# Softmax over 16,384 rows on one core: group 4's scaling split in two on GpSimd, store 0 waiting for the first part

## The chip, the core and the metric

The kernel runs on one core of one Trainium2 chip. Its compute engines here are VectorE (DVE in the profile), ScalarE (ACT) and GpSimd (POOL); TensorE does nothing. SyncE (SP) only waits for semaphores and issues the DMAs, all on one queue, whose transfers are spread over the core's 16 DMA engines. The metric is the time of one execution on the device in microseconds; the kernel before took 159.41 us in the median of three runs (159.51, 159.41, 159.30).

## The reference

```python
x = randn(16, 1024, 512)  # float32

def reference(x):
    x_max = np.max(x, axis=-1, keepdims=True)
    exp_x = np.exp(x - x_max)
    return exp_x / np.sum(exp_x, axis=-1, keepdims=True)
```

It is a softmax over the last axis, in float32: 16 x 1024 = 16,384 rows of 512 numbers. 33.55 MB are read and as many written.

## The kernel before

The 16,384 rows stand as 128 rows of 512 numbers on each of 128 partitions. A *group* is 8 such rows (128 x 4096 numbers, 2 MB), so there are 16 groups, 0 to 15. All data lives in one tensor `held` in SBUF, a ring with room for 12 groups (line 16): groups 12 to 15 take the places of groups 0 to 3 once these are stored. What is loaded is changed in place and stored from there.

**Transfers.** The DMAs move *blocks* (line 21): of 16 rows, two groups, 4 MB, and one of 32 rows (64 to 95, groups 8 to 11), 8 MB. A load or store is named here by its first row: load 64 brings rows 64 to 95, store 0 takes rows 0 to 15, groups 0 and 1. `ORDER` (line 22) writes the order of all 14 transfers out by hand: loads 0, 16, 32, 48, 64; stores 0, 16, 32; loads 96, 112; stores 48, 64, 96, 112. SP issues them in this order on a single queue. The first five loads are issued at once. Ahead of every further one, lines 142 to 157 put waits: a store waits until the groups in it are scaled (one semaphore per group, `scaled[g]`); a load that reuses a place in the ring waits for the store that empties it; and `AFTER` (line 42) adds to four of them a wait for one more group. In this kernel store 0 has to wait for group 4, though it holds groups 0 and 1 only, load 96 for group 8, load 112 for group 9 and store 48 for group 11. A group that has been waited for once isn't waited for again (`done`). As SP takes its instructions in order, whatever stands behind a waiting one waits as well.

**Compute.** For each group g there are three steps.

- M: VectorE takes the maximum of each row, negated, into `shift` (line 168), after the load that brings the group.
- ScalarE computes exp(x + shift) row by row, eight instructions per group, and sums each row into `sums` (line 212).
- P or V: VectorE computes 1/sums (line 176), and the group is multiplied by it (line 182), on GpSimd for groups 0 to 11 (P) and on VectorE for groups 12 to 15 (V). The multiplication is a single instruction over 8 rows, `recip` broadcast along each row, and raises `scaled[g]` at its end.

`VECTOR` (line 46) gives the order of the steps on VectorE, written out by hand; GpSimd takes its groups in order, each after its reciprocal is there.

The one line of waits that the change touches:

```python
AFTER = {("S", 0): 4, ("L", 96): 8, ("L", 112): 9, ("S", 48): 11}
```

Of the kernel before, what the change touches and what calls it, by code (L numbers as in the profile page):

```python
# [13 lines left out]
GROUP = 8  # L14
# [24 lines left out]

AFTER = {("S", 0): 4, ("L", 96): 8, ("L", 112): 9, ("S", 48): 11}

# [28 lines left out]
@with_exitstack  # L74
def kernel(
    ctx: ExitStack,
    tc: tile.TileContext,
    x: bass.AP,
    out: bass.AP,
):  # L80
    nc = tc.nc
    nc.at_finalize(loads_at_the_head)
    P = nc.NUM_PARTITIONS

    d = x.shape[-1]
    x_rows, out_rows = x.flatten_outer_dims(), out.flatten_outer_dims()
    assert x_rows.shape[0] == GROUPS * GROUP * P

    def in_dram(rows, a, b):

        first, last = next(k for k in BLOCKS if k[0] <= a and b <= k[1])
        block = rows[first * P : last * P].rearrange("(p r) d -> p r d", p=P)
        return block[:, a - first : b - first, :]

    held = nc.alloc_sbuf_tensor("held", [P, RING, d], F32).ap()
    shift = nc.alloc_sbuf_tensor("shift", [P, GROUPS * GROUP], F32).ap()
    sums = nc.alloc_sbuf_tensor("sums", [P, GROUPS * GROUP], F32).ap()
    recip = nc.alloc_sbuf_tensor("recip", [P, GROUPS * GROUP], F32).ap()

    loads = [k for what, k in ORDER if what == "L"]  # L100
    stores = [k for what, k in ORDER if what == "S"]
    loaded = {k: nc.alloc_semaphore(f"loaded{k[0]}") for k in loads}
    scaled = [nc.alloc_semaphore(f"scaled{g}") for g in range(GROUPS)]
    stored = {k: nc.alloc_semaphore(f"stored{k[0]}") for k in stores}
    maxed = nc.alloc_semaphore("maxed")
    expd = nc.alloc_semaphore("expd")
    to_pool = nc.alloc_semaphore("to_pool")
    to_vector = nc.alloc_semaphore("to_vector")

    def take(engine, semaphore, n):  # L110

        engine.wait_ge(semaphore, n).then_inc(semaphore, -n)  # L112

    def rows(a, b):
        assert a // RING == (b - 1) // RING
        return held[:, a % RING : (b - 1) % RING + 1, :]

    def meets(k, a, b):
        return k[0] < b and a < k[1]

    def group(g):
        return g * GROUP, (g + 1) * GROUP

    def stats(t, g):
        return t[:, g * GROUP : (g + 1) * GROUP]

    def load(k):
        copy = nc.sync.dma_start(out=rows(*k), in_=in_dram(x_rows, *k))
        copy.then_inc(loaded[k], 16)
        return copy  # L130

    with tc.manual_schedule():
        for _, k in ORDER[:AHEAD]:
            tc.no_tile_sem_insts.add(load(k).ins.name)
    tc.close()
    tc.compile()  # L139

    taken, done = set(), set()
    for what, k in ORDER[AHEAD:]:
        for g in range(GROUPS):
            due = AFTER.get((what, k[0])) == g or (what == "S" and meets(k, *group(g)))
            if due and g not in done:
                take(nc.sync, scaled[g], 1)
                done.add(g)
        if what == "L":
            for s in stores:
                if meets(s, k[0] - RING, k[1] - RING) and s not in taken:  # L150
                    take(nc.sync, stored[s], 16)
                    taken.add(s)
            load(k)
        else:
            nc.sync.dma_start(out=in_dram(out_rows, *k), in_=rows(*k)).then_inc(
                stored[k], 16
            )

    seen, given = set(), {}

    def rowmax(g):
        for k in loads:
            if meets(k, *group(g)) and k not in seen:
                take(nc.vector, loaded[k], 16)
                seen.add(k)
        nc.vector.reduce_max(  # L168
            out=stats(shift, g), in_=rows(*group(g)), axis=AX, negate=True
        ).then_inc(maxed, 1)  # L170

    def scale(g, engine, ready):

        if g == 0:
            take(nc.vector, expd, 1)
        ratio = nc.vector.reciprocal(out=stats(recip, g), in_=stats(sums, g))  # L176
        if g:
            ratio.wait_op(expd, g, "sem-ge")
        ratio.then_inc(ready, 1)
        if g == 0:  # L180
            take(engine, ready, 1)
        product = engine.tensor_mul(  # L182
            out=rows(*group(g)),
            in0=rows(*group(g)),
            in1=stats(recip, g).unsqueeze(2).to_broadcast([P, GROUP, d]),
        )
        if g:
            given[ready] = given.get(ready, 0) + 1
            product.wait_op(ready, given[ready], "sem-ge")
        product.then_inc(scaled[g], 1)  # L190

    for step in VECTOR.split():
        what, g = step[0], int(step[1:])
        if what == "M":
            rowmax(g)
        elif what == "V":
            scale(g, nc.vector, to_vector)
        else:
            scale(g, nc.gpsimd, to_pool)
    take(nc.vector, expd, GROUPS - 1)  # L200
    take(nc.vector, to_vector, given[to_vector])
    take(nc.gpsimd, to_pool, given[to_pool])


    nc.scalar.preload_act_table(EXP)  # L205

    with nc.scalar.Fori(0, GROUPS) as i:  # L207
        take(nc.scalar, maxed, 1)
        for r in range(GROUP):
            row = held[:, bass.ds(i % (RING // GROUP) * GROUP + r, 1), :]  # L210
            at = bass.ds(i * GROUP + r, 1)
            act = nc.scalar.activation(  # L212
                out=row,
                in_=row,
                func=EXP,
                bias=shift[:, at],
                scale=1.0,
                accum_out=sums[:, at],
            )
        act.then_inc(expd, 1)  # L220


    for k in stores:
        if k not in taken:
            take(nc.sync, stored[k], 16)
# [30 lines left out]
```

## Time and profile before

| what | us |
|---|---|
| median of three timed runs | 159.41 |
| the profiled execution, its whole time | 159.34 |
| its span, first to last instruction | 158.0 |
| VectorE / ScalarE / GpSimd busy | 90.0 / 92.1 / 83.9 |
| one scaling of 128 x 4096 on GpSimd (line 182) | 7.018 |
| the same on VectorE | 4.424 |
| one row maximum of 128 x 4096 on VectorE (line 168) | 4.398 |
| one exp of 128 x 512 on ScalarE (line 212) | 0.707 |
| issue of store 0 / load 96 / load 112 / store 48 on SP | 58.56 / 86.53 / 93.50 / 107.38 |

The span is what the profile covers; around it lie another 1.3 us that belong to the execution's time. Times such as 58.56 count from the span's start. "Busy" is the time in which an engine has an instruction running. A DMA's issue is a short instruction on SP (shown as SPq); the transfer itself runs later, on the DMA engines, behind what was issued before it, and "to landing" is the time from the issue until its semaphore shows that all is there. Each of the 16 DMA engines moves its share of a transfer in packets of 32 KB (64 KB for the block of 32 rows); the trace has a start and a duration for every packet.

### The profile page before, as it was taken

The page shows a single profiled execution, that of the slowest core. Times are in us where ns is not written, and L with a number is a line of the kernel's source. Part 1 is how long each engine was busy: PE and PEld are TensorE (multiplying, and loading weights), DVE is VectorE, ACT ScalarE, POOL GpSimd, SP SyncE. Part 2 cuts the span into 40 slices and gives each one's busy share as a digit, 9 for nine tenths or more (in the row PEclk, how much of TensorE's full clock was granted, in tenths as well). Part 3 has the DMA queues.
Part 4 walks back from the last instruction along what each step waited for, and adds up shares of the span by engine and source line. Part 5 has one row for each costly group of instructions (what it writes and reads, how often), then busy time and mean ns, then how long its engine had stood idle before and what let it go on. Part 6 is the DMA issues. An engine that isn't in the chain of part 4 may idle for free. (4 is left out here: it accounts for less than half of the span.)

```text
span 158.0 us, 716 instructions
## 1 busy us (share of the span) xinstructions
DVE 90.0 (57%) x36; ACT 92.1 (58%) x257; POOL 83.9 (53%) x16
## 2 busy tenths in 40 slices
DVE  0008959778877915969770000695999996920000
ACT  1100699999999998399999300049946839000000
POOL 0000009999999999999999999991000000000000
DMA  8999999999969979999999999999999969999996
GB/s 265 423 481 423 398 456 465 406 415 481 564 265 531 481 315 398 423 481 423 398 448 465 406 406 398 415 498 415 398 448 481 531 265 531 390 406 406 465 456 265
DMA packets 2016, 67.11 MB, mean 425 GB/s; under 512 B 224, under 2 KB 224, under 8 KB 224
## 3 DMA queue, kind: packets, MB, share of 16 engines
q1 hardware_dynamic: 2016, 67.11, 99.1%
HBM read 33.55 MB, written 33.55 MB: 425 GB/s over the span
## 5 line engine op out<-in xcount | busy, mean ns | idle before, releaser
L212 ACT ACTIVATE held<-held,shift x128 | 90.4, 707 | 39.0 <-ACTq L112 39.0
L182 POOL TENSOR_TENSOR held<-held,recip 128x4096 f32<-128x4096 f32 x12 | 83.7, 7018 | 23.1 <-POOLq L112 23.1
L168 DVE TENSOR_REDUCE shift<-held 128x8 f32<-128x4096 f32 x16 | 70.2, 4398 | 27.7 <-DVEq L112 27.7
L212 ACT ACTIVATION_READ_ACCUMULATOR held<-held,shift x128 | 23.9, 187 | 0.0
L182 DVE TENSOR_TENSOR held<-held,recip 128x4096 f32<-128x4096 f32 x4 | 17.7, 4424 | 0.1
L176 DVE RECIPROCAL recip<-sums 128x8 f32<-128x8 f32 x16 | 3.2, 201 | 21.4 <-ACT held L212 19.5
L205 ACT ACT_TABLE_LOAD x1 | 1.3, 1283 | 3.4 <-PEq L139 3.4
L240 POOL MEMSET const-float32-0.0<- 128x1 f32 x1 | 0.1, 99 | 0.2 <-issue 0.2
L240 POOL MEMSET const-bfloat16-1.0<- 128x1 bf16 x1 | 0.1, 102 | 0.0
L240 POOL MEMSET const-uint8-127<- 128x1 uint8 x1 | 0.1, 102 | 0.0
L240 POOL MEMSET const-float32-1.0<- 128x1 f32 x1 | 0.1, 99 | 0.0
## 6 DMA issues: line engine op xcount, KB each, us to landing
held<-in_x_dram SPq DMA_DIRECT2D x6, 4096.0 KB, 18.7
out_dram<-held SPq DMA_DIRECT2D x6, 4096.0 KB, 19.8
held<-in_x_dram SPq DMA_DIRECT2D x1, 58.5
out_dram<-held SPq DMA_DIRECT2D x1, 30.8
```

The lines of the kernel that those rows point to most:

```text
L168: nc.vector.reduce_max(out=stats(shift, g), in_=rows(*group(g)), axis=AX, negate=True).then_inc(maxed, 1)
L176: ratio = nc.vector.reciprocal(out=stats(recip, g), in_=stats(sums, g))
L182: product = engine.tensor_mul(out=rows(*group(g)), in0=rows(*group(g)), in1=stats(recip, g).unsqueeze(2).to_broadcast([P, GROUP, d]),)
L205: nc.scalar.preload_act_table(EXP)
L212: act = nc.scalar.activation(out=row, in_=row, func=EXP, bias=shift[:, at], scale=1.0, accum_out=sums[:, at],)
L240: nc = _bacc.Bacc("TRN2", target_bir_lowering=False, num_devices=1)
```

## The change

Group 4's scaling on GpSimd becomes two instructions: one over its first seven rows, which raises a new semaphore, `begun`, and one over its eighth row, which raises `scaled[4]` as before. Store 0 waits for `begun` (and for groups 0 and 1, which it holds) in place of `scaled[4]`. The wait for `scaled[4]` now stands ahead of store 32, which holds groups 4 and 5. All other groups are scaled by one instruction, all other waits and the order of the transfers are the same.

```diff
-AFTER = {("S", 0): 4, ("L", 96): 8, ("L", 112): 9, ("S", 48): 11}
+
+AFTER = {("L", 96): 8, ("L", 112): 9, ("S", 48): 11}
+AFTER_FIRST = {("S", 0): 4}
+FIRST = {4: 7}
...
+    begun = nc.alloc_semaphore("begun")
...
+        if (what, k[0]) in AFTER_FIRST:
+            take(nc.sync, begun, 1)
         if what == "L":
...
-        product = engine.tensor_mul(
-            out=rows(*group(g)),
-            in0=rows(*group(g)),
-            in1=stats(recip, g).unsqueeze(2).to_broadcast([P, GROUP, d]),
-        )
+        def multiply(a, b):
+            return engine.tensor_mul(
+                out=rows(a, b),
+                in0=rows(a, b),
+                in1=recip[:, a:b].unsqueeze(2).to_broadcast([P, b - a, d]),
+            )
+
+        first, last = group(g)
+        lead = FIRST.get(g, GROUP)
+        product = multiply(first, first + lead)
         if g:
             given[ready] = given.get(ready, 0) + 1
             product.wait_op(ready, given[ready], "sem-ge")
+        if lead < GROUP:
+            product.then_inc(begun, 1)
+            product = multiply(first + lead, last)
         product.then_inc(scaled[g], 1)
```

## The prediction

> **What bounds the kernel now.** I read the page's head, busy shares and DMA queue first.
>
> ```profile
> span 158.0 us, 716 instructions
> DVE 90.0 (57%) x36; ACT 92.1 (58%) x257; POOL 83.9 (53%) x16
> ...
> DMA  8999999999969979999999999999999969999996
> ...
> q1 hardware_dynamic: 2016, 67.11, 99.1%
> ```
>
> No engine is busy over 58% of the span; the 16 DMA engines are, at 99.1%. The digits 6 and 7 within the DMA line are not idle time: some packets last 2.4 us and are booked whole, so shares move between neighbouring slices. The packet records settle that: a 32 KB packet takes 1.213 us, a 64 KB one 2.418, and on every engine the next packet begins 3 to 20 ns after the last one's end, across the borders between transfers too. At those durations 67.11 MB are 96 x 1.213 + 16 x 2.418 = 116.4 + 38.7 = 155.1 us on each engine (three quarters of the bytes in 32 KB packets; one quarter, load and store of rows 64 to 95, in 64 KB ones). The first packet starts at 1.02 us and the last ends at 157.6, which is 156.6; packets longer than normal fill the rest: 0.74 us per engine in the first packet of all, 0.51 us per engine between 88 and 94 us, where loads follow stores, and 0.1 us anywhere else. So the end moves only if a transfer reaches its engines after the one ahead of it is through, or if packets get longer or shorter.
>
> Then the issues and landings (start, duration of the issue; the line after it gives issue to landing), from the timeline of SP and the DMA answer for the same stretch:
>
> ```profile
> 58.56 0.35 SPq L155 DMA_DIRECT2D out_dram<-held  x1
> out_dram<-held SPq DMA_DIRECT2D x1, 4096.0 KB, 11.9
> 59.09 0.34 SPq L155 DMA_DIRECT2D out_dram<-held  x1
> out_dram<-held SPq DMA_DIRECT2D x1, 4096.0 KB, 21.0
> 86.53 0.34 SPq L128 DMA_DIRECT2D held<-in_x_dram  x1
> held<-in_x_dram SPq DMA_DIRECT2D x1, 4096.0 KB, 13.4
> 107.38 0.34 SPq L155 DMA_DIRECT2D out_dram<-held  x1
> out_dram<-held SPq DMA_DIRECT2D x1, 4096.0 KB, 12.0
> ```
>
> The first pair is store 0, then store 16, load 96, store 48. By the packet records load 64 (the one ahead of store 0) ends between 59.68 us on the earliest engine and 60.31 on the latest, and store 0's first packets start 4 to 7 ns after that on each engine. So store 0 came in time: 1.11 us from issue to first packet, no hole. The very first load, with nothing ahead of it, shows 1.02 us on its first engine and 1.39 on its last. Store 48 is alike: issued at 107.38, its packets start from 108.66 (earliest) to 109.27 (latest), right behind load 112.
>
> Last the GpSimd rows, the whole kernel and a stretch of it:
>
> ```profile
> 23.55 83.74 POOL L182 TENSOR_TENSOR held<-held,recip 128x4096 f32<-128x4096 f32 x12 [23.11 <-POOLq L112]
> 44.47 27.94 POOL L182 TENSOR_TENSOR held<-held,recip 128x4096 f32<-128x4096 f32 x4
> L240 POOL MEMSET const-bfloat16-1.0<- 128x1 bf16 x1 | 0.1, 102 | 0.0
> ```
>
> Twelve scalings run without a pause, 83.74 / 12 = 6.98 us apart (each lasts 7.018, so neighbours overlap by 0.04). The stretch begins with group 3; group 4 runs 51.45 to 58.47, and store 0 is issued 0.09 us after.
>
> **The change part by part.**
>
> *Store 0's wait.* Seven of eight rows are done 6.98 / 8 = 0.87 us sooner, at about 57.60, so store 0 is issued at 57.69 and store 16, next on SP, at 58.22. Store 16 is not needed before 69.36, where store 0 ends, so its move is worth nothing. Store 0's lead over the earliest engine's need grows from 1.11 to 1.98 us. What can that bring? Its packets already start where load 64's end; its first packets are 7.6 ns per engine longer than 1.213 us in sum (the worst 33 ns). I take a gain of 0.01 us. What it can cost is not in the trace: both stores that follow loads were issued 1.11 and 1.28 us ahead, neither with harm. The nearest row is load 96, issued 2.44 us before the stores ahead of it end, and that border costs 0.51 us per engine. Bounds: 0.01 gained to 0.51 lost. I take nothing lost, because store 0's row and store 48's are of the same direction (store behind load) and load 96's is not, and the cold first load pays 0.74 us as well, so that loss looks like that of beginning to read.
>
> *SP's waits.* One wait for `begun` takes the place of the one for group 4 ahead of store 0; that for group 4 moves ahead of store 32, together with that for group 5. A further wait that is already met takes 0.07 us (two such waits stand at 58.958 and 59.024). Store 32 was issued at 65.53 and its packets begin at 79.0: covered by 12 us. Nothing else is behind it until load 96, which waits for group 8.
>
> *The split on GpSimd.* The elements are the same, so the price d is that of one more instruction. Every later scaling (5 to 11) starts d later, since there is no idle time on GpSimd to absorb it. Lower bound: 0.0 (the memsets start 0.03 to 0.04 us apart and neighbours overlap by as much). Upper bound: 2.6 us, if GpSimd's rate per element were as good as that of VectorE, whose same operation takes 4.42 us, and all the rest of the 7.02 were a fixed price. I take 0.1, from the memset of one element per partition, 0.102 us, the smallest thing this engine runs. Cover: store 32 (group 5) 12 us; load 96 (group 8) is issued at 86.53 + d and needed at 88.97, less 1.11 for the way is 1.33; load 112 (group 9) is issued at 93.50 + d and needed at 98.97, 4.4 left; store 48 (group 11) is issued at 107.38 + d and needed at 108.66, which leaves 1.28 - 1.11 = 0.17 on the earliest engine. The end is set by the latest engine, which needs store 48 only at 109.27: 0.77 us left if its packets come 1.11 after the issue, 0.49 if 1.39. So d = 0.1 is hidden at all of them; without cover it would be 0.1 us in 158.
>
> The GPSIMD Engine Reference of the Trainium skill ("Performance versus the Vector engine", the table of measured operations) speaks against this part: it gives 4497 ns for a two-input operation on 2048 fp32 elements. A straight line through that figure and our 7.018 us for 4096 has a fixed part of 2 x 4497 - 7018 = 1976 ns, by which d would be an estimated 2.0 us and the time 160.6 to 160.9; its own account of 2.6 cycles per element has next to no fixed part, and no row here has a second size. The sum goes by the memset row.
>
> *Sum.* 158.0 - 0.01 + 0 + 0 (0.1 hidden) = 158.0 us of span. Around the span lie 159.34 - 158.0 = 1.3 us, giving 159.3; that execution is 0.07 under the median of the timed runs, 159.41. On the median: 159.4.
>
> **The rivals.**
>
> *Faster: store 0 comes late in the timed executions.* The 1.11 us that store 0 has is only 0.09 more than the 1.02 that the first load needed, and its first packets are up to 33 ns long, as if they had barely made it. If the way takes longer outside the profile, all engines stand still, and 0.87 us of lead removes up to that much: half of it gives 159.41 - 0.44 = 159.0. Against: no engine shows a hole, and the profiled execution, 159.34, is not faster than the timed ones, 159.30 to 159.51.
>
> *Slower, by the queue: a store that waits longer behind running loads disturbs them.* The lead of 1.98 us lies outside the 1.28 us known to be harmless and short of the 2.44 at which a border (of the other direction) costs 0.51. From some lead above 1.28 it would cost up to that: 159.6 to 159.9. Against: five loads stand in the queue from 2.7 us on and their packets keep 1.213; stores 16 and 32 wait 10 and 13 us behind other stores at no cost. But no store ever waited that long behind a load here.
>
> *Slower, by GpSimd: one more instruction costs much more than a memset.* It decides from d = 0.5 to 0.77 on, where store 48 reaches even the latest engine too late, and everything behind it moves by the rest. At the upper bound, 2.6, that is 1.8 to 2.1 us: 161.2 to 161.5; at half of it, 1.3, some 0.5 to 0.8: 159.9 to 160.2. The late load 96 (1.27 us at d = 2.6 on the earliest engine) doesn't come on top: it moves the need for store 48 along. For it: not one row with another size shows the fixed price. Against: 0.04 us of overlap between neighbours, which a large start-up price would hardly leave.
>
> *The change doesn't do it:* if GpSimd reported the seven rows only with the eighth, store 0 would be issued when it is now, and the time would be the forecast's; it needs no chance of its own.
>
> **How the numbers follow.** No change 0.47, with 159.1 to 159.7 as its own range (0.2% of 159.4 is 0.32 us, which is about what a measurement of this kernel can tell from no change). Store 0 late until now 0.22, 158.5 to 159.1. The queue 0.18, 159.6 to 159.9 and mostly beyond the 0.2%. GpSimd 0.13, 159.9 to 161.5. Faster 0.22, within 0.2% 0.47, slower 0.18 + 0.13 = 0.31. The time is the first case's, 159.4. From 158.8 to 160.4 I leave out the lower half of the faster case (0.11) and two thirds of GpSimd's (0.09), 0.20 together; as cases of both signs have over half of the chance between them, the likeliest one's own range above should be read beside it.
>
> **What would show it.** Store 0 issued near 57.7 and not 58.56: the release works. Its packets still 3 to 20 ns behind load 64's, first packets at 1.213: nothing was to be gained. Load 64's last packets, 2.418 now, longer: the queue rival. The start of group 5's scaling, 58.43 now, gives d, as do the issues of load 96 (86.53) and store 48 (107.38), which must move by the same d; holes ahead of store 48's packets near 109 mean GpSimd's rival. The forecast is wrong if the DMA engines' extra time (0.51 us at 88 to 94, 0.1 elsewhere) grows or shrinks by more than 0.3 us, at whichever border.

## The result and the profile after

The changed kernel takes 160.38 us in the median of four runs (159.77 to 160.50) against 159.40 before; the ratio is 1.0048 with a 95% interval of 1.0028 to 1.0069. It is slower, by 0.5%. The execution that left the first trace is the shortest of its four, 159.77 us, so it shows only part of the loss.

The head, the DMA rows and GpSimd's groups by shape (busy us, mean ns, idle before) of the changed kernel:

```profile
span 158.5 us, 718 instructions
...
DMA  7999999999969969999999999999997998999996
...
q1 hardware_dynamic: 2016, 67.11, 98.7%
```

```profile
L189 POOL TENSOR_TENSOR held<-held,recip 128x4096 f32<-128x4096 f32 x11 | 76.8, 7015 | 23.1 <-POOLq L116 23.1
L189 POOL TENSOR_TENSOR held<-held,recip 128x3584 f32<-128x3584 f32 x1 | 6.2, 6161 | 0.0
L189 POOL TENSOR_TENSOR held<-held,recip 128x512 f32<-128x512 f32 x1 | 1.0, 1037 | 0.0
```

The span is 0.5 us longer and the DMA engines' share falls from 99.1 to 98.7%: same bytes, some idle time. With three sizes GpSimd's price can be read: 512 elements more cost 7015 - 6161 = 854 ns, so of the 1037 ns of the small instruction 0.18 us are fixed. Neighbours overlap by 0.04, and group 5 begins at 58.56 instead of 58.42 us: d = 0.14 us.

The issues on SP and their landings, as shown of before (store 0, store 16, load 96, and the last store, 112):

```profile
57.70 0.35 SPq L161 DMA_DIRECT2D out_dram<-held  x1
out_dram<-held SPq DMA_DIRECT2D x1, 4096.0 KB, 12.7
58.24 0.34 SPq L161 DMA_DIRECT2D out_dram<-held  x1
out_dram<-held SPq DMA_DIRECT2D x1, 4096.0 KB, 21.9
86.67 0.34 SPq L132 DMA_DIRECT2D held<-in_x_dram  x1
held<-in_x_dram SPq DMA_DIRECT2D x1, 4096.0 KB, 13.5
139.63 0.33 SPq L161 DMA_DIRECT2D out_dram<-held  x1
out_dram<-held SPq DMA_DIRECT2D x1, 4096.0 KB, 18.8
```

The same of store 112 before:

```profile
139.40 0.33 SPq L155 DMA_DIRECT2D out_dram<-held  x1
out_dram<-held SPq DMA_DIRECT2D x1, 4096.0 KB, 18.6
```

Store 0 is issued 0.86 us sooner and lands at 57.70 + 12.7 = 70.4 us, where 58.56 + 11.9 = 70.5 was before: nothing gained. Load 96 lands at 100.2 instead of 99.9, store 112 at 158.4 instead of 158.0. So the loss begins between the landings of store 0 and load 96.

The packet records say where. Every engine has eight data packets for each transfer; here are the border from store 32 to load 96 and the end of store 112, over the 16 engines (us; the hole is the pause ahead of load 96's first packet; "longer" is the sum over 1.213 us per packet):

```
                        before           changed
store 32, longer        0.07 mean        0.01 mean
hole before load 96     0.00, max 0.00   0.07, max 0.62
load 96, first packet   0.18, max 0.54   0.26, max 0.78
load 96, the others     0.28, max 0.64   0.11, max 0.60
load 96 ends            98.98 to 99.59   98.80 to 99.82
store 112 ends, mean    157.36           157.37
store 112 ends, last    157.63           158.08
```

The mean engine loses nothing: 157.37 against 157.36. But before, each engine paid between 0.1 and 0.9 us on load 96; now four pay nothing and one pays 1.2 us. As each engine has its fixed share of every transfer, such a difference stays to the end, and the slowest engine sets the time: 158.08 against 157.63 is the whole 0.45 us of the span. Of this, 0.23 us is there when load 96 ends (99.82 against 99.59). The other 0.22 us is added on the same engine by its last packet of load 112, which takes 1.43 us and not 1.21, while other engines are already writing store 48; before, no packet of load 112 is longer. Around store 0 the two kernels are alike to 0.01 us (its packets start within 7 ns of load 64's end on every engine).

### The profile page after: what moved, and what is told of

Same layout as the page of the kernel before. It is cut to its first block, busy times and chain, and to the rows that moved or that the text cites. A ratio compares the mean times of both kernels' runs of the same rounds, so it can differ in the third digit from the quotient of the medians.

```text
span 158.5 us, 718 instructions
## 1 busy us (share of the span) xinstructions
DVE 90.0 (57%) x36; ACT 92.1 (58%) x257; POOL 84.1 (53%) x17
## 3 DMA queue, kind: packets, MB, share of 16 engines
q1 hardware_dynamic: 2016, 67.11, 98.7%
## 5 line engine op out<-in xcount | busy, mean ns | idle before, releaser
L189 POOL TENSOR_TENSOR held<-held,recip 128x4096 f32<-128x4096 f32 (+2 forms) x13 | 83.9, 6490 | 23.1 <-POOLq L116 23.1
```

The source lines that it names most:

```text
L189: return engine.tensor_mul(out=rows(a, b), in0=rows(a, b), in1=recip[:, a:b].unsqueeze(2).to_broadcast([P, b - a, d]),)
```

## Experiments

Four theories were tried one against the other: A, the 0.14 us that the split puts on load 96 and what follows; B, store 0's earlier issue; then whether shifts simply add up (T), or whether the moments of store 0 and load 96 belong together (S, P).

**The change again, and its two parts apart.** `e0_after` is the changed kernel once more. `e1_split5` has the 0.14 us without the earlier store 0:

```diff
-AFTER = {("L", 96): 8, ("L", 112): 9, ("S", 48): 11}
-AFTER_FIRST = {("S", 0): 4}
-FIRST = {4: 7}
+AFTER = {("S", 0): 4, ("L", 96): 8, ("L", 112): 9, ("S", 48): 11}
+AFTER_FIRST = {}
+FIRST = {5: 7}
...
-            product.then_inc(begun, 1)
```

`e2_short5` has the earlier store 0 and gives the 0.14 us back in group 5, by leaving the last 10 numbers of each of its rows unscaled:

```diff
+COLUMNS = {5: 502}
...
+            n = COLUMNS.get(g, d)
...
-                out=rows(a, b),
-                in0=rows(a, b),
+                out=rows(a, b)[:, :, :n],
+                in0=rows(a, b)[:, :, :n],
-                in1=recip[:, a:b].unsqueeze(2).to_broadcast([P, b - a, d]),
+                in1=recip[:, a:b].unsqueeze(2).to_broadcast([P, b - a, n]),
```

`e3_mark` takes the kernel before and releases store 0 from VectorE, with no split:

```diff
-AFTER = {("S", 0): 4, ("L", 96): 8, ("L", 112): 9, ("S", 48): 11}
+AFTER = {("L", 96): 8, ("L", 112): 9, ("S", 48): 11}
...
+        if (what, k[0]) == ("S", 0):
+            take(nc.sync, begun, 1)
...
+        if step == "M8":
+            nc.vector.memset(mark, 0.0).then_inc(begun, 1)
```

> The changed kernel again, beside the kernel before on the same chip. The first look at it had three executions at 160.36 to 160.50 and one at 159.77, and only the last one's trace. Both theories expect 160.2 to 160.5 in most executions. What the trace of such an execution must show: store 0's packets still 3 ns behind load 64's on all engines, and the loss at the border between store 32 and load 96 (88 to 94 us) or later; a trace in which the loss lies at store 0 would speak for the theory that store 0's earlier issue costs it.

> Group 5 is split 7 + 1 and not group 4, and store 0 waits for the whole group 4 as in the kernel before: store 0 at 58.56 us as before, but everything GpSimd does from group 6 on 0.14 us later, load 96 at 86.67, load 112 at 93.64, store 48 at 107.52. Theory A (the 0.14 us on load 96, or on what follows it, costs the time): 160.2 to 160.5. Theory B (store 0's earlier issue costs it): 159.3 to 159.5.

> The changed kernel, but group 5 is scaled over 502 of its 512 columns (the last 10 numbers of each row stay unscaled), which takes 0.13 us off GpSimd: store 0 at 57.70 us as in the changed kernel, load 96 at 86.53, load 112 at 93.50 and store 48 at 107.38 as in the kernel before. Theory A: 159.3 to 159.5. Theory B: 160.2 to 160.5.

> The kernel before with store 0 released early in another way: not by GpSimd, whose groups stay whole, but by a small memset on VectorE behind group 6's reciprocal, while VectorE has nothing to do. Store 0 near 57.5 us, load 96 at 86.53 and store 48 at 107.38 as in the kernel before. Theory A: 159.3 to 159.5. Theory B: 160.2 to 160.5.

Measured: `e0_after` 160.16 us (159.39 to 160.91, six runs), ratio 1.0052 [1.0033, 1.0072]; `e1_split5` 159.78, 1.0018 [1.0009, 1.0027]; `e2_short5` 159.77, 1.0020 [1.0006, 1.0033]; `e3_mark` 159.76, 1.0023 [1.0012, 1.0035]. Neither A nor B held: each part alone costs about 0.3 us, and the two together 0.7 to 1.0. Each run left one trace, so where its loss lies is read from a single execution. The trace of `e0_after` is of its shortest execution, 159.39, and can't show the loss. Those of the others put it where the first one did: load 64's packets are the same to 0.01 us, and load 96 ends within 0.55 us from first to last engine in `e1_split5`, where all of them pay more (0.61 us longer packets in the mean, 0.46 before), but within 1.45 us in `e2_short5` and 1.36 in `e3_mark`, where single engines stand still for up to 1.1 us ahead of it.

**Each of the two issues further, one at a time.** `f1_store0_g3` changes one number, `("S", 0): 3`. `f2_load96_early` splits group 8 and releases load 96 by its first seven rows (`AFTER_FIRST = {("L", 96): 8}`, `FIRST = {8: 7}`, store 0 back to group 4). `f3_load96_late` and `f4_store0_late` delay one issue on SP by waits that are already met:

```diff
+PAUSE = {("L", 96): 4}
...
+        for _ in range(PAUSE.get((what, k[0]), 0)):
+            take(nc.sync, pause, 1)
...
+    for n in range(sum(PAUSE.values())):
+        nc.vector.memset(mark[:, n : n + 1], 0.0).then_inc(pause, 1)
```

> The kernel before, with store 0 waiting for group 3 in place of group 4: store 0 at 51.6 us, 7.0 us earlier than before (0.87 us in the changed kernel), load 96 at 86.53 as before. If what an earlier store 0 costs grows with its lead, 160.5 or more; if it is one step, reached as soon as store 0 comes sooner than at 58.56, 159.7 to 159.8 as with the memset on VectorE; if the rise of 0.33 us there had another cause than store 0, 159.3 to 159.5. The loss should again lie at the border from store 32 to load 96, in the slowest engine more than in the mean of the 16.

> Group 8 is split 7 + 1 and load 96 waits for its first seven rows; store 0 waits for group 4 as in the kernel before. Load 96 at 85.67 us, 0.86 earlier than before; load 112 and store 48 0.14 later (93.64, 107.52). Theory A1 (the later load 96 itself costs the 0.35 us seen with group 5 split, because it leaves less lead over the end of store 32): 159.4 or less. Theory A2 (it is load 112 or store 48 coming 0.14 later): 159.7 to 159.8.

> The kernel before, with four further waits on SP, already met, ahead of load 96 alone: load 96 some 0.27 us later, at 86.80; store 0, load 112 and store 48 as before. Theory A1: 159.8 to 160.2, more than with 0.14 us, and the loss at the border from store 32 to load 96. Theory A2: 159.3 to 159.5.

> The kernel before, with the four further waits ahead of store 0: store 0 at 58.83 us, 0.27 later than before, store 16 at 59.36; load 96 at 86.53. On the engines that end load 64 first (59.68) store 0 may come up to 0.25 us late, which the slowest engine (60.31) does not feel. If the cost goes with store 0's lead in steps below 1 us, 159.3 or less, with less spread than before; if only a lead over 1.1 us matters, 159.4.

Measured: 160.30 us (1.0057 [1.0044, 1.0070]), 160.19 (1.0049 [1.0033, 1.0066]), 160.71 (1.0078 [1.0055, 1.0100]), 160.03 (1.0045 [1.0032, 1.0058]). The two with pauses carry 0.4 us more outside the span, so spans are compared below: 159.0, 158.9, 159.0 and 158.3 against 158.1. Theory A1, by which only a late load 96 costs, is out: it costs when it is 0.3 us later, and also when it is 0.86 earlier. (In `f2_load96_early` load 112 and store 48 come 0.14 us later as well; in `g1_both_early` below that costs nothing.) So is A2: load 96 alone, with nothing else moved, cost 0.9 us of span. A later store 0 is no gain either.

`f1_store0_g3` was expected to lose at the border to load 96. It loses elsewhere. Its rows for load 64, store 0, store 32 and load 96 (the last number of a landing row is issue to landing):

```profile
2.17 0.46 SPq L128 DMA_DIRECT2D held<-in_x_dram  x1
held<-in_x_dram SPq DMA_DIRECT2D x1, 59.4
51.67 0.35 SPq L155 DMA_DIRECT2D out_dram<-held  x1
out_dram<-held SPq DMA_DIRECT2D x1, 4096.0 KB, 19.6
65.61 0.33 SPq L155 DMA_DIRECT2D out_dram<-held  x1
out_dram<-held SPq DMA_DIRECT2D x1, 4096.0 KB, 25.3
86.60 0.34 SPq L128 DMA_DIRECT2D held<-in_x_dram  x1
held<-in_x_dram SPq DMA_DIRECT2D x1, 4096.0 KB, 13.9
```

Load 64 and store 32 before:

```profile
2.21 0.44 SPq L128 DMA_DIRECT2D held<-in_x_dram  x1
held<-in_x_dram SPq DMA_DIRECT2D x1, 58.5
65.53 0.33 SPq L155 DMA_DIRECT2D out_dram<-held  x1
out_dram<-held SPq DMA_DIRECT2D x1, 4096.0 KB, 24.4
```

Load 64 lands at 2.17 + 59.4 = 61.6 us; before it was issued at 2.21 and landed 58.5 later, at 60.7. The packet records show that the last packet of load 64 on every engine takes 2.96 to 3.78 us and not 2.42 (0.93 more in the mean): a store that stands 8 us behind loads does disturb them. And load 96 lands 100.5 - 90.9 = 9.6 us after store 32, against 99.9 - 89.9 = 10.0 before: the border that cost 0.5 us per engine before is free here. Load 96 was issued at its old time by the clock, but as load 64 delayed the stores by 0.9 us, it came that much earlier against store 32.

That gave a clue. Store 32's last packets are prolonged (0.05 to 0.44 us per engine in the mean) in all traces with store 0 at its old moment or later, and not (0.01) in the traces with an earlier store 0 and load 96 at 86.5 or later. So store 0's moment has an effect on the border 30 us behind it.

**Both moved together.** `g1_both_early` is the changed kernel with `FIRST = {4: 7, 8: 7}` and load 96 released by group 8's first part; `g2_both_earlier` has 6 + 2 rows; `g3_load96_g7` is the kernel before with `("L", 96): 7`; `g4_store0_alone` is `e3_mark` with `("S", 16): 4` in `AFTER`, so that store 16 doesn't move with store 0.

> The changed kernel with group 8 split 7 + 1 as well and load 96 waiting for its first seven rows: store 0 at 57.70 us as in the changed kernel, load 96 at 85.81 and not 86.67. Theory S (an earlier store 0 leaves the stores in a state in which store 32's last packets aren't prolonged, as in all five traces with an early store 0, and load 96 pays nothing if it comes some 3 us ahead, as with store 0 released by group 3): span 157.5 to 158.0, time 158.8 to 159.3. Theory T (any shift of one of the two issues away from the kernel before costs, and shifts add up): 160.3 or more.

> The same with splits of 6 + 2 rows in groups 4 and 8: store 0 near 56.84 us, load 96 near 84.95. Theory S: 158.8 to 159.3 unless load 64's last packets are now prolonged (0.93 us per engine with store 0 at 51.67, 0.01 with 57.70), which would make it up to 160.2. Theory T: 160.3 or more.

> The kernel before with load 96 waiting for group 7 in place of group 8: load 96 at 79.5 us, 7 us earlier, store 0 at 58.56 as before. If a load queued long behind stores prolongs their last packets as a store did behind loads: store 32's last packets 0.5 to 1 us longer on all engines, load 96's own normal, 159.4 to 160.2. If load 96 pays for a start of reading whenever it comes, 159.4.

> Store 0 released early by the memset on VectorE, near 57.7 us, but store 16 waits for group 4 and is issued at 58.56 (59.09 before). If store 0's own lead makes the difference: 159.7 to 159.8, and store 32's last packets at 1.213 us. If it is store 16's, which the changed kernel moved as well: 159.4, and store 32's last packets prolonged by 0.05 us per engine or more, as in the traces with store 0 at 58.56 or later.

Measured: `g1_both_early` 159.46 us, 1.0002 [0.9994, 1.0011]; `g2_both_earlier` 159.70, 1.0018 [1.0007, 1.0029]; `g3_load96_g7` 159.85, 1.0043 [1.0026, 1.0060]; `g4_store0_alone` 160.28, 1.0054 [1.0033, 1.0076]. `g1_both_early` has the changed kernel's early store 0 and its split, with a second one on top, and the loss is gone; theory T, which wanted 160.3, is out. It isn't the gain that S hoped for. `g2_both_earlier` begins to lose at load 64, whose last packets are 0.38 us longer in the mean and 0.95 at most. In `g3_load96_g7` it is store 32's last packets that are longer, by 0.36 us in the mean. `g4_store0_alone` shows that store 0's own lead is enough, without store 16's; why it costs 0.9 us there and 0.3 in `e3_mark`, on another chip, is not shown.

The same rows, store 32 and load 96, of `g4_store0_alone` and then of `g1_both_early`:

```profile
65.57 0.33 SPq L158 DMA_DIRECT2D out_dram<-held  x1
out_dram<-held SPq DMA_DIRECT2D x1, 4096.0 KB, 24.4
86.56 0.34 SPq L129 DMA_DIRECT2D held<-in_x_dram  x1
held<-in_x_dram SPq DMA_DIRECT2D x1, 4096.0 KB, 14.2
```

```profile
65.71 0.33 SPq L161 DMA_DIRECT2D out_dram<-held  x1
out_dram<-held SPq DMA_DIRECT2D x1, 4096.0 KB, 24.3
85.84 0.34 SPq L132 DMA_DIRECT2D held<-in_x_dram  x1
held<-in_x_dram SPq DMA_DIRECT2D x1, 4096.0 KB, 14.0
```

Store 32 lands at 90.0 in both. With load 96 at 86.56 us, 10.8 us pass until it lands; with 85.84, 9.8. Both have store 0 at 57.7. The packet records of `g4_store0_alone` have engines that end load 96 at 98.62 and others at 100.44; in `g1_both_early` the last is at 99.46.

**Is it the difference alone?** `h1_both_late` has `PAUSE = {("S", 0): 4, ("L", 96): 4}`; `h2_marks` releases both early from VectorE, with no split; its main addition to `e3_mark` is:

```diff
+        if step == "P11":
+            nc.vector.memset(mark[:, 512:], 0.0).then_inc(begun, 1)
```

> The kernel before with four further waits on SP, already met, ahead of store 0 and four ahead of load 96: both some 0.28 us later against the transfers in hand. Measured apart, the later store 0 gave a median span of 158.3 us and the later load 96 one of 159.0, against 158.1 before (these kernels carry 0.4 us more outside the span, so spans are compared). Theory P (the best moment for load 96 moves with that of store 0, so that only their difference counts): 158.0 to 158.3. Theory T (each shift costs by itself): 159.1 or more.

> Store 0 released early by the memset on VectorE (near 57.7 us) and load 96 as well, by a longer one behind group 10's reciprocal (near 85.7 us). No scaling is split and GpSimd runs as in the kernel before, so load 112 and store 48 stay at 93.50 and 107.38. Theory P: 159.2 to 159.5, as with both released by seven rows of their groups (159.46), where load 112 and store 48 came 0.14 us later. Theory T: 160.2 or more.

Measured: spans of 158.3 us (158.2 to 158.4) and 158.1 (157.9 to 158.3), times of 159.90 (1.0021 [1.0012, 1.0030]) and 159.68 (1.0007 [0.9998, 1.0017]). The times carry 0.3 us more outside the span than the kernel before; which of the added instructions costs that is not shown. `h2_marks` missed its 159.2 to 159.5 by that alone. Load 96 later alone cost 0.9 us of span; with store 0 later as well, 0.2 is left, what the later store 0 costs alone. Load 112 and store 48 at their old moments (`h2_marks`) or 0.14 later (`g1_both_early`) make no difference.

All together, by the shift of the two issues in us against the transfers in hand, as the edits set it (the traces agree within 0.2 us); for `f1_store0_g3` load 96's shift is that of its trace:

| kernel | store 0 | load 96 | median span | range |
|---|---|---|---|---|
| before | 0 | 0 | 158.1 | 157.8 to 158.8 |
| changed (first runs and e0) | -0.87 | +0.14 | 158.95 | 158.1 to 159.6 |
| e1_split5 | 0 | +0.14 | 158.45 | 158.1 to 158.7 |
| e2_short5, e3_mark | -0.87 | 0 | 158.45, 158.4 | 158.1 to 159.0 |
| g4_store0_alone | -0.87 | 0 | 159.0 | 158.4 to 159.9 |
| f4_store0_late | +0.28 | 0 | 158.3 | 158.1 to 158.6 |
| f3_load96_late | 0 | +0.28 | 159.0 | 158.1 to 159.5 |
| f2_load96_early | 0 | -0.86 | 158.9 | 158.3 to 159.4 |
| g3_load96_g7 | 0 | -7 | 158.55 | 158.2 to 159.3 |
| g1_both_early | -0.87 | -0.7 | 158.1 | 157.9 to 158.3 |
| h2_marks | -0.9 | -0.6 | 158.1 | 157.9 to 158.3 |
| h1_both_late | +0.28 | +0.28 | 158.3 | 158.2 to 158.4 |
| g2_both_earlier | -1.7 | -1.6 | 158.4 | 158.2 to 158.7 |
| f1_store0_g3 | -7 | -0.9 | 159.0 | 158.9 to 159.1 |

Shifts of one issue cost 0.2 to 0.9 us of span; shifts of both in the same direction cost 0 to 0.3, as long as store 0 doesn't come so early that load 64 pays 0.9 us (`f1_store0_g3`). The difference isn't the whole law: `g1_both_early` widens it by 0.17 us and `h2_marks` by 0.3 at no cost, `e1_split5` by 0.14 at 0.35. No version beats the kernel before.

## Why the prediction was wrong

*The bound* was right: nothing but the DMA engines' time counts, and store 0's packets had no hole ahead of them to close. Nothing was gained there, as the sum had it.

*The price of the split* was right in kind: d = 0.14 us, where the memset's 0.10 was taken. The GpSimd rival needed 0.5 and is out. By the straight line through the 4497 ns that the GPSIMD Engine Reference of the Trainium skill gives ("Performance versus the Vector engine") d would have been an estimated 2.0 us. The measurement decides: 0.18 us fixed, less the overlap, and 1.67 ns per element, which is neither that line nor the 2.6 cycles per element that the same section of the Trainium skill gives (2.2 ns at the 1.2 GHz it reckons with).

*The step that failed* is "I take nothing lost" for store 0's greater lead, and beside it "d = 0.1 is hidden at all of them", as far as load 96 goes. The early store 0 by itself cost 0.32 us (`e2_short5`), 0.37 (`e3_mark`, 0.0023 x 159.4) and 0.86 (`g4_store0_alone`), so that even the bound of 0.51 lost was too narrow; the 0.14 us cost 0.29 (`e1_split5`). Together they are 0.7 to 1.0 between the medians. The error was to ask of each transfer only whether it comes before the engines need it. Load 96 had 1.33 us to spare by that measure, and yet 0.29 us was lost when it and what follows came 0.14 later, and 0.9 us of span when it alone came 0.3 later.

*The range*, 158.8 to 160.4, just holds the measured 160.38, but that is luck: its upper end came from the GpSimd rival, which is out. The case that was taken as likeliest, 159.1 to 159.7, doesn't hold it.

*The queue rival* had the sign, too small a size (159.6 to 159.9) and the wrong place. A store that waits behind loads does prolong them: load 64's last packets by 0.93 us per engine with 8 us of lead and by 0.38 with 2.7, but by nothing with the changed kernel's 2.0. What that lead changes is how evenly the loads behind the stores start, 30 us later. The 0.22 us in load 112's last packet on the slowest engine, with store 48 waiting behind it, may be the rival's effect after all; the slowest engine shows the same with 0.57 us in `f3_load96_late` and 0.18 in `e3_mark`, but none in `e2_short5`, and no run moves store 48 alone, so this is not shown.

*The test named in advance* looked at the extra time summed over the engines, and that sum doesn't show the loss: longer packets are 1.19 us per engine after and 1.34 before. It is the spread between engines that grew. The prediction gave 0.51 us per engine as the price of the border, a mean, where the slowest engine counts: it was 0.27 us behind the mean at the end before, 0.72 after, 0.92 in `e3_mark` and 1.38 in `g4_store0_alone`.

*Two readings of the packet records* were a little off. Within a transfer a packet's record mostly begins 3 to 5 ns before the last one's end, and not 3 to 20 ns after it. And 156.6 us runs from the first engine's start to the last engine's end; one engine takes 156.2 in the mean. Store 48 was not harmless everywhere either: before, one engine waited 0.15 us for it. None of this reaches the slowest engine.

*What stays open* is how store 0's moment reaches the border 30 us later. The Trainium skill says (DMA: Bandwidth & Descriptors, "Two DMAs through the same engine are not ordered") that an engine's read and write sides are separate queues and descriptors are pipelined. With this, an earlier store 0 could let the reading side run further ahead of the writing side through all three stores, so that load 96's reads are due earlier as well; load 64's last packets, prolonged only when store 0 is issued 2.7 us or more ahead of its turn, would fit. The records show one start and one duration for each packet and not its two sides, so this is argued and not shown.

## What to carry to other kernels

In this kernel, where the DMA engines are busy all the time, a change from loads to stores or back has a price that depends on how long before its turn the next transfer was issued, and earlier is not safer: too early prolongs what runs (0.93 us per engine in `f1_store0_g3`), too late makes single engines stand still (up to 0.4 us in `f3_load96_late`). Elsewhere it has to be measured. Moments that were set to suit each other have to be moved together and measured together. Read such a border engine by engine: the last one sets the end, and a mean over 16 hides it.

## What the runs showed that was not expected

A store issued 8 us ahead of its turn made the last load packet of every engine 0.5 to 1.4 us longer (2.96 to 3.78 us instead of 2.42), and the next start of loads behind stores then cost nothing (9.6 us between the landings of store 32 and load 96). At that border single engines stood still for up to 1.1 us (`e2_short5`) while their neighbours read on without a pause.

The kernel before is steady, 159.1 to 159.9 us in all but one of the 89 runs beside the experiments, while the changed one scatters from 159.4 to 160.9 with the same instructions. The first packet of the very first load, which nothing precedes, starts between 1.0 us on the first engine and 1.4 to 2.1 on the last, different in each trace.
